# Hybrid encoder layer on one core: the triangular solve, the recurrence and the gates each run one attention later, and the weighted sums one tile later

## The chip, the cores and the metric

The kernel runs on one core of one Trainium2 chip. The metric is the device time of one execution in microseconds (us), lower is better; the time of a kernel is the median of its runs. TensorE (PE) multiplies, VectorE (DVE) and ScalarE (ACT) do the elementwise work, GpSimd (POOL) does a little and issues DMAs, SyncE (SP) issues the other DMAs and the transposes that go through DMA.

## The reference

One layer of a hybrid streaming encoder over T = 1088 tokens (1024 prompt tokens and 64 sample tokens), D = 1024. Four branches read one projection `u @ w_in`: fox (attention with a forgetting bias), diff (difference of two softmaxes), sb (stick-breaking attention: a reversed cumulative sum over the keys) and gdn (gated DeltaNet: a unit-triangular solve in each 64-token chunk, then a recurrence over the chunks). Their outputs are gated and merged, and an output projection and a feed-forward network follow.

```
x = x + W_out( sum_b sigmoid(gate_b(u)) * P_b(branch_b(u)) ),  u = rms_norm(x)
x = x + swiglu(rms_norm(x));  y = rms_norm(x)
# gdn: sol = triangular_solve(m + I, rhs) of every chunk; then, chunk after chunk,
v_new = u_i - kc_i @ S
o     = (q_i * exp(g_i)) @ S + a_i @ v_new
S     = S * exp(g_last) + (k_i * exp(g_last - g_i))^T @ v_new
```

The outputs are y, the new keys and values of the three attentions, and the new state of gdn, for both token groups.

## The kernel before

Every large product is made of f16 pairs (a high and a low part), so it costs three matmuls. The tokens are cut into 9 tiles of at most 128 rows; an attention goes over 2 pairs of heads and, in each, over the tiles in the order `QORD` (7, 6, 5, 4, 3, 2, 8, 1, 0), the longest rows of keys first. For one tile the sequence is: load the queries (`load_q`, a DMA transpose), score matmuls (`scores`, tile `psc`), softmax or stick-breaking on ACT and DVE, a DMA transpose of the probabilities (`p_tiles`, `pt<-st`, line 447), then the weighted sums (`pv_pair`, tile `pv`, lines 462 to 473; in diff `diff_out`, tile `po`).

Between the scores and the weighted sums of a tile the code calls `fill(us)` (lines 503 to 515). It takes other work from two lists. `dense` holds matmul work that waits for nothing: units of 24 matmuls, either of a projection (tile `pd`, lines 165 to 167, 256 columns each) or of a gate (tile `pgs`, lines 183 to 185, up to 364 columns each, copied out by ACT as `ths` and written to memory). There are 96 gate units, in 16 generators' worth of weights. `side` holds a chain of small steps: `gdn_solve` (lines 861 to 890, 30 steps of forward substitution on DVE, tiles `X` and `tmpx`) or `gdn_seq` (lines 896 to 1040, the recurrence over 17 chunks: for each tile a preparation, `py` to `kc`, and for each chunk `vn`, `vh`, `pds`, `S`, `Sh`, `Sl`, `pks`, then `pog` and `osg`, which goes to memory as `od_gdn`).

The stages before: sb attention, with the rest of the fox projection and the diff projection as fill and the solve as side chain; fox attention, with gates as fill and the recurrence as side chain; diff attention, with the rest of the gates as fill. The merges follow: for each branch its outputs (`oT`), its weights (`wbh`, `wbl`) and 24 products (`ptb`) that are multiplied by the tanh of the gates (`thg`) and added up. Their pool `brp` is opened before diff attention. Then come the output projection and the feed-forward network, which the change does not touch.

The order in which an engine gets its instructions is not that of the code: a scheduler simulates a timeline and places them. A statement inside `tc.issue_after(x)` is placed no earlier than x.

## Time and profile before

| | us |
|---|---|
| median of 3 runs | 1852.74 (1850.4 to 1865.82) |
| the profiled execution | 1846.53 |
| its span | 1844.7 |
| PE busy | 1731.3 (94%) |
| DVE busy | 1253.2 (68%) |
| ACT busy | 864.1 (47%) |
| first score of sb / fox / diff | 301.4 / 489.5 / 640.4 |
| last gate matmul, last merge matmul | 957.7, 1064.7 |

The profiled execution lies 1.8 us beside its span and 6.2 us under the median. The last two lines are points in the timeline of the trace, counted from the start of the span. A busy TensorE is not one at its peak: matmuls are pipelined, and the records overlap, so the granted clock and the time from start to start have to be read beside the busy time.

### The profile page before, as it was taken

The page shows a single profiled execution, that of the slowest core. Times are in us where ns is not written, and L with a number is a line of the kernel's source. Part 1 is how long each engine was busy: PE and PEld are TensorE (multiplying, and loading weights), DVE is VectorE, ACT ScalarE, POOL GpSimd, SP SyncE. Part 2 cuts the span into 40 slices and gives each one's busy share as a digit, 9 for nine tenths or more (in the row PEclk, how much of TensorE's full clock was granted, in tenths as well). Part 3 has the DMA queues.
Part 4 walks back from the last instruction along what each step waited for, and adds up shares of the span by engine and source line. Part 5 has one row for each costly group of instructions (what it writes and reads, how often), then busy time and mean ns, then how long its engine had stood idle before and what let it go on. Part 6 is the DMA issues. An engine that isn't in the chain of part 4 may idle for free.

```text
span 1844.7 us, 36720 instructions
## 1 busy us (share of the span) xinstructions
PE 1731.3 (94%) x14364; PEld 1226.5 (66%) x14364; DVE 1253.2 (68%) x2589; ACT 864.1 (47%) x1819; POOL 302.9 (16%) x445
## 2 busy tenths in 40 slices
PE   7999887798898899999998899999999999999997
PEld 5678775675565566666565588777758668577573
DVE  7558874899766576877757886757546456465455
ACT  6335555888755554655646533423314224132132
POOL 2113221001222222232334620000000000000002
PEclk9999998899999999999999999999999999999999
DMA  6267689989899975664949746412212112112113
GB/s 227 50 107 200 209 245 167 217 185 208 181 193 214 191 154 143 147 163 102 251 133 285 209 132 108 101 52 58 70 35 78 37 48 81 35 35 69 35 47 103
DMA packets 412157, 244.60 MB, mean 133 GB/s; under 512 B 266146, under 2 KB 389502, under 8 KB 411916
## 3 DMA queue, kind: packets, MB, share of 16 engines
q1 hardware_dynamic: 398944, 205.67, 47.1%
q0 software_dynamic: 13040, 36.60, 7.4%
q8 instruction: 112, 1.84, 0.4%
q14 instruction: 61, 0.50, 0.1%
HBM read 123.39 MB, written 60.81 MB: 100 GB/s over the span
## 4 chain that ended last, share of the span: by engine, by line
PE 66%; DMA 13%; DVE 11%; issue 5%; ACT 3%; POOL 1%; SPq 1%; DVEq 0%; POOLq 0%; ACTq 0%
PE po L1432 12%; PE pgs L185 5%; PE pgs L183 5%; PE pgs L184 5%; DMA pt<-st 4%; PE pb L1316 3%; PE pb L1315 3%; PE pb L1317 3%; PE pc L1316 2%; PE pc L1317 2%; PE pa L1317 2%; PE pc L1315 2%; PE pa L1316 2%; PE pa L1315 2%; PE psc L456 2%
## 5 line engine op out<-in xcount | busy, mean ns | idle before, releaser
L183 PE MATMUL pgs<-u,wh 128*128 128x364 f16 (+1 forms) x768 | 245.3, 319 | 2.7 <-ACT ths L61 2.7
L185 PE MATMUL pgs<-u,wl 128*128 128x364 f16 (+1 forms) x768 | 245.5, 320 | 0.0
L184 PE MATMUL pgs<-u,wh 128*128 128x364 f16 (+1 forms) x768 | 245.4, 320 | 0.0
L1432 PE MATMUL po<-wh,hT 128*128 128x512 f16 (+1 forms) x792 | 238.1, 380 | 0.6 <-DVE x2a L64 0.6
L1432 PEld LDWEIGHTS <-hT 128*128 128x128 f16 (+1 forms) x1188 | 109.2, 99 | 120.0 <-issue 7.6
L64 DVE SCALAR_TENSOR_TENSOR x2a<-po,x2a 128x512 f32<-128x512 f32 x108 | 74.5, 690 | 140.2 <-PE po L1432 140.0
L61 ACT ACTIVATE wh<-w32f 128x1024 f16<-128x1024 f32 (+1 forms) x90 | 80.3, 926 | 160.6 <-PE po L1432 111.7
L1315 PE MATMUL pb<-X,wh 128*128 128x288 f16 (+1 forms) x528 | 147.1, 279 | 2.5 <-DMA X<-nsh 2.2
L64 DVE SCALAR_TENSOR_TENSOR wl<-w32f,wh 128x1024 f16<-128x1024 f32 (+1 forms) x90 | 94.7, 1066 | 79.8 <-ACT wh L61 79.7
L1316 PE MATMUL pb<-X,wh 128*128 128x288 f16 (+1 forms) x528 | 147.2, 279 | 0.3 <-DMA X<-nsl 0.3
L1317 PE MATMUL pb<-X,wl 128*128 128x256 f16 (+1 forms) x528 | 146.3, 279 | 0.0
L1432 PE MATMUL po<-wl,hT 128*128 128x512 f16 (+1 forms) x396 | 142.0, 379 | 0.0
L1315 PEld LDWEIGHTS <-wh 128*128 128x128 f16 x1232 | 120.5, 98 | 31.0 <-issue 2.3
L1316 PEld LDWEIGHTS <-wh 128*128 128x128 f16 x1232 | 120.5, 98 | 30.0 <-issue 2.4
L1317 PEld LDWEIGHTS <-wl 128*128 128x128 f16 x1232 | 120.5, 98 | 27.2 <-issue 0.9
L165 PE MATMUL pd<-wh,u 128*128 128x256 f16 (+1 forms) x448 | 125.6, 280 | 4.0 <-DVE qs L64 2.6
L167 PE MATMUL pd<-wh,u 128*128 128x256 f16 (+1 forms) x448 | 125.0, 279 | 0.0
L166 PE MATMUL pd<-wl,u 128*128 128x256 f16 (+1 forms) x448 | 125.0, 279 | 0.0
L184 PEld LDWEIGHTS <-wh 128*128 128x128 f16 x912 | 89.8, 98 | 51.9 <-issue 4.1
L185 PEld LDWEIGHTS <-wl 128*128 128x128 f16 x912 | 89.6, 98 | 51.0 <-issue 2.6
L183 PEld LDWEIGHTS <-wh 128*128 128x128 f16 x912 | 89.7, 98 | 50.4 <-issue 1.5
L71 POOL TENSOR_SCALAR fss<-fss 128x1 f32<-128x1 f32 (+1 forms) x9 | 2.0, 219 | 660.3 <-ACT fsq L1461 660.3
(393 smaller groups left out, 4642.7 us busy)
## 6 DMA issues: line engine op xcount, KB each, us to landing
w<-in_w_in_dram SPq DMA_DIRECT2D x56, 512.0 KB, 4.8
w32f<-in_w_ffn_gate_dram SPq DMA_DIRECT2D x20, 512.0 KB, 5.0
w32f<-in_w_ffn_up_dram SPq DMA_DIRECT2D x20, 512.0 KB, 4.0
w32f<-in_w_ffn_down_dram SPq DMA_DIRECT2D x20, 512.0 KB, 4.0
xt<-in_x_prompt_dram SPq DMA_DIRECT2D x8, 512.0 KB, 6.8
wb<-in_w_branch_dram SPq DMA_DIRECT2D x8, 512.0 KB, 4.8
w<-in_w_out_dram SPq DMA_DIRECT2D x8, 512.0 KB, 5.8
x2a<-in_x_prompt_dram SPq DMA_DIRECT2D x8, 512.0 KB, 6.7
```

Of the source, the lines that this page charges most:

```text
L61: return act.activation(out, in_, AF.Copy, scale=scale)
L64: return vec.scalar_tensor_tensor(out=out, in0=in0, scalar=s, in1=in1, op0=op0, op1=op1)
L165: pe.matmul(ps[:n, :N], lhsT=a, rhs=wh[:, k, :N], start=(k == 0), stop=False)
L166: pe.matmul(ps[:n, :N], lhsT=a, rhs=wl[:, k, :N], start=False, stop=False)
L167: pe.matmul(ps[:n, :N], lhsT=b, rhs=wh[:, k, :N], start=False, stop=(k == K - 1))
L183: pe.matmul(ps[:, :n], lhsT=a, rhs=xh[:, k, off:off + n], start=(k == 0), stop=False)
L184: pe.matmul(ps[:, :n], lhsT=a, rhs=xl[:, k, off:off + n], start=False, stop=False)
L185: mm = pe.matmul(ps[:, :n], lhsT=b, rhs=xh[:, k, off:off + n], start=False, stop=(k == K - 1))
L1315: pe.matmul(ps[:, :n], lhsT=wh[:, k], rhs=xh_, start=(start and k == 0), stop=False, skip_group_check=not start)
L1316: pe.matmul(ps[:, :n], lhsT=wh[:, k], rhs=xl_, start=False, stop=False, skip_group_check=not start)
L1317: mm = pe.matmul(ps[:, :n], lhsT=wl[:, k], rhs=xh_, start=False, stop=(k == 3), skip_group_check=not start)
L1432: pe.matmul(ps[h * n:h * n + n], lhsT=hts[k + h][:, a, tk:tk + n], rhs=w[:, k + h], start=(k == 0 and a == 0 and w is wh), stop=(k + nh >= ...
```

## The change

Three things change.

- The weighted sums of a tile are held back (`behind_scores`) and issued behind the last score matmul of the next tile; there are 6 buffers for transposed probabilities instead of 4, and `tiles_of` requests the queries of the next tile, and the keys and values of the next pair, one tile ahead.
- The side work moves one attention on. Sb attention is filled with the rest of the fox projection and gates and has no side chain; fox attention is filled with the diff projection and gates and has the solve; diff attention has the rest of the gates and the recurrence. The merges' pool is opened only when the recurrence's pool has been closed.
- The matrix that the solve reads, `nd`, is stored in three 32 by 32 blocks: 51 smaller writes instead of 17, and one contiguous load instead of two strided ones.

```diff
-FILL_SB, FILL_FOX, FILL_DIFF, FILL_GDN = 0.0143, 0.006, 0.0155, 8
+FILL_SB, FILL_FOX, FILL_DIFF, FILL_GDN = 0.0143, 0.0085, 0.0155, 8
...
-        pt = at.tile([P, 16, P], F16, tag="pt", name="pt", bufs=4)
+        pt = at.tile([P, 16, P], F16, tag="pt", name="pt", bufs=6)
...
+    def tiles_of(b):
+
+        units = [(pair, t) for pair in range(2) for t in QORD]
+        kv, q = {}, {}
+        for k in range(len(units)):
+            for m in range(k, min(k + 2, len(units))):
+                pair, t = units[m]
+                if pair not in kv:
+                    kv[pair] = load_kv(b, pair)
+                if m not in q:
+                    q[m] = load_q(b, pair, t, rows(t))
+            pair, t = units[k]
+            yield pair, t, q.pop(k), kv[pair]
+
+    held = []
+
+    def behind_scores(mm, run):
+
+        if held:
+            with tc.issue_after(mm.ins) if mm is not None else ExitStack():
+                held.pop()()
+        if run is not None:
+            held.append(run)
...
-        for pair in range(2):
-            kT, vt = load_kv("sb", pair)
-            for t in QORD:
+        for pair, t, qt, (kT, vt) in tiles_of("sb"):
                 n, kc, W, vl = qgeom(t)
-                qt = load_q("sb", pair, t, n)
                 pts = []
...
-                    sb_mark[0] = stt(sv[:n, 1, :W], z[:n, :W], PS, sv[:n, 0, :W], ALU.mult, ALU.subtract)
+                    stt(sv[:n, 1, :W], z[:n, :W], PS, sv[:n, 0, :W], ALU.mult, ALU.subtract)
                     pts.append(tr())
+                behind_scores(mm, lambda a=(pair, t, n, vt, vl, pts): pv_pair("sb", *a))
                 fill(FILL_SB * W)
-                pv_pair("sb", pair, t, n, vt, vl, pts)
+        behind_scores(None, None)
 
...
+                    at_mark[0] = stt(sv[:n, 1, :W], s[:n, :W], mn[:n, 3:4], sv[:n, 0, :W], ALU.mult, ALU.subtract)
                     pts.append(tr())
+                behind_scores(mm, lambda a=(pair, t, n, vt, vl, pts): pv_pair("fox", *a))
                 fill(FILL_FOX * W)
-                pv_pair("fox", pair, t, n, vt, vl, pts)
+        behind_scores(None, None)
 
...
+                    behind_scores(mm, lambda a=(pair, t, n, nb, vl, vt, hp, pt, o32): diff_out(*a))
                     fill(FILL_DIFF * W / 2)
-                    diff_out(pair, t, n, nb, vl, vt, hp, pt, o32)
+        behind_scores(None, None)
...
-    nd = tc.dram_tile([18, NH, 64, 64], F32, name="nd")
+    nd = tc.dram_tile([18, NH, 3, 32, 32], F32, name="nd")
...
-                gps.dma_start(nd[2 * t + c].rearrange("h j i -> j h i"), n32[64 * c:64 * c + 64])
+                for b, (j0, i0) in enumerate(((0, 0), (32, 32), (0, 32))):
+                    gps.dma_start(nd[2 * t + c, :, b].rearrange("h j i -> j h i"),
+                                  n32[64 * c + j0:64 * c + j0 + 32, :, i0:i0 + 32])
...
-            for q in range(2):
-                sl = slice(32 * q, 32 * q + 32)
-                gps.dma_start(X[:, q], nd[0:17, :, sl, sl].rearrange("n h j i -> (n h) j i"))
+            gps.dma_start(X.rearrange("p b j i -> p b (j i)"), nd[0:17, :, 0:2].rearrange("n h b j i -> (n h) b (j i)"))
...
-                behind = tc.issue_after(sb_mark[0].ins) if j == 1 else ExitStack()
+                behind = tc.issue_after(at_mark[0].ins) if j == 1 else ExitStack()
...
-    def spill_gates(b, sp):
+    def spill_gates(b, sp, d2):
...
-        dense += proj
+        dense += proj[0:2]
...
-        side.append(gdn_solve())
+        dense += [spill_gates(b, sp, d2) for b in gtd for d2 in range(4)]
         attend_sb()
-    drain(dense)
-    drain(side)
-    pj_.close()
+    drain(dense, proj[1])
+    drain(dense, dense[0])
     cb_ = ExitStack()
     cb = cb_.enter_context(tc.tile_pool(name="cb", bufs=1, side="right", reuse_waits="tile"))
+    dense.insert(0, proj[2])
+    side.append(gdn_solve())
+    attend_fox()
+    drain(dense, proj[2])
+    drain(side)
+    cb_.close()
+    pj_.close()
     gd_ = ExitStack()
     g3 = gd_.enter_context(tc.tile_pool(name="gp3", bufs=1, side="right", reuse_waits="tile"))
-    dense += [spill_gates(b, sp) for b in gtd]
     side.append(gdn_seq(g3))
-    attend_fox()
+    attend_diff()
     drain(side)
     gd_.close()
-    cb_.close()
+    drain(dense)
+    ap_.close()
     br_ = ExitStack()
     brp = br_.enter_context(tc.tile_pool(name="br", bufs=1, side="right", reuse_waits="tile"))
-    attend_diff()
-    drain(dense)
-    ap_.close()
```

Counted in the order of the changed kernel, 5 gate units stand before sb's first score, 31 between sb's first and last score, 5 in fox attention and the other 55 behind diff's first score. Three places show the move.

VectorE, in the middle of sb attention of the kernel before (`cu`, `z` and `st` are a head's stick-breaking, `X` and `tmpx` the solve, `ks` the projection of diff's keys):

```order
L541 SCALAR_TENSOR_TENSOR cu_4536<-cu_4536,e_4535 128x512
L64 SCALAR_TENSOR_TENSOR st_4310<-z_4291,st_4310 128x640
L67 TENSOR_TENSOR tmpx_3733<-X_3732 68x60
L67 TENSOR_TENSOR z_4534<-z_4534,cu_4536 128x512
L71 TENSOR_SCALAR cu_4556<-z_4554 128x512
L64 SCALAR_TENSOR_TENSOR os_4261<-pv_4224,os_4261 128x128
L67 TENSOR_TENSOR X_3732<-X_3732,tmpx_3733 68x2x30
L67 TENSOR_TENSOR tmpx_3733<-X_3732 68x116
L64 SCALAR_TENSOR_TENSOR ks_4778<-e32_4775,ks_4778 128x8x32 x2
L67 TENSOR_TENSOR X_3732<-X_3732,tmpx_3733 68x2x2x29
```

and VectorE of the changed kernel, where the solve begins, in fox attention (`ISA` is fox's row maximum, `s` and `st` its softmax):

```order
L64 SCALAR_TENSOR_TENSOR st_6906<-s_6892,mn_6893,st_6906 128x640
L67 TENSOR_TENSOR tmpx_6483<-X_6482 68x60
L64 SCALAR_TENSOR_TENSOR st_7036<-s_7026,mn_7027,st_7036 128x512
L67 TENSOR_TENSOR X_6482<-X_6482,tmpx_6483 68x2x30
L64 SCALAR_TENSOR_TENSOR ks_7013<-e32_7010,ks_7013 128x8x32 x2
L67 TENSOR_TENSOR tmpx_6483<-X_6482 68x116
L591 ISA s_7165,mn_7166<-psc_7167,ckb_6308 128x384
L591 ISA mn_7166 128x1
L591 ISA s_7180,mn_7181<-psc_7182,ckb_6308 128x384
L591 ISA mn_7181 128x1
```

The solve's steps and the copies of diff's projection stand between the softmax steps of fox and no longer between those of sb.

TensorE at the end of the recurrence, before (`pog` is its last output, `psc` scores of diff, `pgs` a gate):

```order
L1017 LDWEIGHTS rec2b_9342
L1017 MATMUL pog_9380<-vh1_6340,rec2b_9342 64x64
L1018 LDWEIGHTS rec2b_9342
L1018 MATMUL pog_9380<-vh1_6340,rec2b_9342 64x64
L456 LDWEIGHTS qt_11871
L456 MATMUL psc_11878<-kT_11160,qt_11871 128x128
L458 LDWEIGHTS identb_75
L458 MATMUL psc_11878<-mk_diff_83,identb_75 128x128
L456 LDWEIGHTS qt_11871
L456 MATMUL psc_11888<-kT_11160,qt_11871 128x512
L184 LDWEIGHTS wh_13076
L184 MATMUL pgs_13226<-u1_103,wh_13076 128x360
```

and TensorE of the changed kernel at its last gate matmuls (`pu` belongs to the recurrence's tile 5; tiles 6 and 7 are still to come):

```order
L183 MATMUL pgs_13790<-u1_103,wh_13640 128x360
L184 LDWEIGHTS wh_13640
L184 MATMUL pgs_13790<-u1_103,wh_13640 128x360
L185 LDWEIGHTS wl_13641
L185 MATMUL pgs_13790<-u1_103,wl_13641 128x360
L456 LDWEIGHTS qt_13060
L456 MATMUL psc_13204<-kT_11714,qt_13060 128x256
L458 LDWEIGHTS identb_75
L458 MATMUL psc_13204<-mk_diff_83,identb_75 128x128
L997 LDWEIGHTS ttbd1_8773
L997 MATMUL pu_11007<-rec1b_11001,ttbd1_8773 128x64
```

No gate is left behind this point: before, gates stood on both sides of the recurrence's end, and now the rest of tile 5 and the whole of tiles 6 and 7 stand behind the last gate, and the first merge product (`ptb`) behind them.

ScalarE at the end of the recurrence, before (`osg` is the recurrence's last output, `wbh` the first merge weights, `p` a softmax of diff):

```order
L61 ACTIVATE ths_13289<-pgs_13264 128x364
L61 ACTIVATE osg_9626<-ztg_9378 128x256
L61 ACTIVATE t32_11855<-po_11842 128x64
L614 ACTIVATE sq_11858<-o32_11655 128x128
L655 ACTIVATE p_11887,sm16_11873<-psc_11888,sm16_11873 128x512
L655 ACTIVATE p_11887,sm16_11873<-psc_11891,sm16_11873 128x128
L61 ACTIVATE ths_13317<-pgs_13292 128x364
L61 ACTIVATE wbh_13807<-wb32_13809 128x1024
L1145 ACT_TABLE_LOAD
L1145 ACTIVATE thg_13817<-thg_13817 128x364
```

and of the changed kernel:

```order
L61 ACTIVATE u0_11653<-pu_11627 128x256
L61 ACTIVATE kc_11655<-pk_11628 128x512
L61 ACTIVATE vh0_8781<-vn_11672 64x256
L61 ACTIVATE Sh_11710<-S32p_8785 128x256
L61 ACTIVATE vh1_8783<-vn_11780 64x256
L1050 ACTIVATE sqo_11852<-pog_11660 128x256
L61 ACTIVATE osg_11860<-ztg_11658 128x256
L61 ACTIVATE wbh_13840<-wb32_13842 128x1024
L61 ACTIVATE wbh_13840<-wb32_13846 128x1024
L61 ACTIVATE wbh_14117<-wb32_14119 128x1024
```

The first merge weights stand behind `osg` of tile 7 in both; now nothing of diff and no gate stands beside them. GpSimd in the changed kernel:

```order
L1060 DMA od_gdn_349<-osg_11581 128x512
L1047 DMA out_p_gdn_state_dram<-S32p_8785 64x4x64
L72 TENSOR_SCALAR sso_11854<-sso_11854 128x4
L67 TENSOR_TENSOR sso_11854<-sso_11854,mhb_79 128x4
L1060 DMA od_gdn_349<-osg_11860 128x512
L1148 DMA oT_13837<-od_sb_342 128x2x1088 x2
L1148 DMA oT_14114<-od_fox_343 128x2x1088 x2
```

The loads of the branch outputs (`oT`) stand behind the write of the last `osg`.

## Rows read from the trace of the kernel before

**Rows 1.** The page: span, part 1 (busy time, share of the span and instructions of each engine) and the engines' shares of the chain that ended last.

```profile
span 1844.7 us, 36720 instructions
...
PE 1731.3 (94%) x14364; PEld 1226.5 (66%) x14364; DVE 1253.2 (68%) x2589; ACT 864.1 (47%) x1819; POOL 302.9 (16%) x445
...
PE 66%; DMA 13%; DVE 11%; issue 5%; ACT 3%; POOL 1%; SPq 1%; DVEq 0%; POOLq 0%; ACTq 0%
...
```

**Rows 2.** Windows by stage, core 0: the stretch, its length, busy us of each engine (instructions), mean granted TensorE clock, DMA share, GB/s. The stretches are: before the first score of sb; sb attention; between; fox attention; between; diff attention to the last gate matmul; the merges.

```profile
...
core 0: us, PE busy (x) PEld busy (x) DVE busy (x) ACT busy (x) POOL busy (x), PEclk, DMA share, GB/s
229.00:301.40 72.40, 57.20 (x524) 49.79 (x522) 41.35 (x78) 35.70 (x76) 18.75 (x25) 0.90 0.95 212
301.40:483.20 181.80, 158.24 (x1466) 113.04 (x1467) 159.48 (x278) 151.29 (x292) 22.87 (x34) 0.94 0.95 197
483.20:489.50 6.30, 6.30 (x61) 3.97 (x60) 5.51 (x13) 5.00 (x17) 1.58 (x3) 1.00 0.84 236
489.50:626.40 136.90, 122.34 (x1365) 78.58 (x1363) 92.04 (x296) 78.87 (x181) 29.48 (x48) 0.95 0.98 194
626.40:640.40 14.00, 12.13 (x125) 8.04 (x124) 5.79 (x16) 5.73 (x18) 3.01 (x5) 1.00 1.03 238
640.40:957.70 317.30, 311.61 (x2780) 203.47 (x2781) 229.49 (x708) 175.79 (x463) 89.19 (x143) 1.00 0.64 154
957.70:1064.70 107.00, 89.76 (x554) 54.24 (x552) 85.51 (x141) 60.75 (x121) 56.91 (x53) 0.98 0.80 234
...
```

**Rows 3.** What TensorE waited for from 229 to 640 us: us in total, times, longest us.

```profile
...
PE pv L468 <- DMA pt<-st: 24.4, 11, 6.7
PE psc L456 <- DMA qt<-qd_sb: 9.9, 1, 9.9
PE psc L456 <- DMA qt<-qd_fox: 5.8, 2, 3.5
...
```

**Rows 4.** ScalarE's groups of instructions in sb attention (301.4 to 483.2 us): busy us, mean ns | idle before.

```profile
...
L61 ACT ACTIVATE e<-pd 128x256 f32<-128x256 f32 (+1 forms) x18 | 6.9, 383 | 0.1
L61 ACT ACTIVATE ks<-e 128x512 f16<-128x512 f32 (+1 forms) x9 | 5.7, 629 | 0.0
L61 ACT ACTIVATE ths<-pgs 128x364 f32<-128x364 f32 (+1 forms) x12 | 5.6, 470 | 2.0 <-PE pgs L185 2.0
L61 ACT ACTIVATE qs<-pd 128x512 f16<-128x512 f32 (+1 forms) x7 | 4.1, 587 | 7.2 <-PE pd L167 7.2
...
```

**Rows 5.** VectorE's groups in the same stretch.

```profile
...
L67 DVE TENSOR_TENSOR X<-X,tmpx 68x60 f32<-68x60 f32 (+14 forms) x30 | 14.6, 488 | 0.1
L67 DVE TENSOR_TENSOR tmpx<-X 68x60 f32<-68x60 f32 (+14 forms) x30 | 14.5, 482 | 0.1
...
L64 DVE SCALAR_TENSOR_TENSOR ks<-e,ks 128x256 f16<-128x256 f32 (+1 forms) x18 | 6.8, 415 | 0.0
L64 DVE SCALAR_TENSOR_TENSOR qs<-pd,qs 128x256 f16<-128x256 f32 (+1 forms) x14 | 5.3, 417 | 5.1 <-ACT qs L61 5.1
...
```

**Rows 6.** TensorE's groups in the same stretch.

```profile
...
L165 PE MATMUL pd<-wh,u 128*128 128x256 f16 (+1 forms) x184 | 52.2, 284 | 2.6 <-DVE qs L64 2.6
...
L183 PE MATMUL pgs<-u,wh 128*128 128x364 f16 (+1 forms) x102 | 32.9, 322 | 2.7 <-ACT ths L61 2.7
...
```

**Rows 7.** TensorE's group of line 183 in diff attention (640.4 to 957.7 us).

```profile
...
L183 PE MATMUL pgs<-u,wh 128*128 128x364 f16 (+1 forms) x506 | 160.5, 317 | 0.0
...
```

**Rows 8.** Timeline of TensorE in the recurrence's last chunk: start us, duration us.

```profile
...
870.44 0.32 PE L183 MATMUL pgs<-u,wh 128*128 128x360 f16 x1
870.59 0.32 PE L184 MATMUL pgs<-u,wh 128*128 128x360 f16 x1
...
873.62 0.48 PE L1011 MATMUL pds<-vh,rec2b 128*128 128x64 f16 x11
...
```

**Rows 9.** Timeline of VectorE about the recurrence's last two chunks: start us, duration us.

```profile
...
863.27 0.41 DVE L64 SCALAR_TENSOR_TENSOR S32p<-pds,S 128x256 f32<-128x256 f32 x1
...
863.80 0.42 DVE L67 TENSOR_TENSOR S<-S32p,eg 128x256 f32<-128x256 f32 x1
...
864.97 0.43 DVE L64 SCALAR_TENSOR_TENSOR Sl<-S32p,Sh 128x256 f16<-128x256 f32 x1
...
869.23 0.43 DVE L64 SCALAR_TENSOR_TENSOR vn<-pks,u 64x256 f32<-64x256 f32 x1 [0.33 <-PE pks L999]
...
870.13 0.42 DVE L67 TENSOR_TENSOR vh<-vn,vh 64x256 f16<-64x256 f32 x1 [0.29 <-ACT vh L61]
...
876.20 0.41 DVE L1032 TENSOR_REDUCE sso<-sqo 128x4 f32<-128x256 f32 x1
...
```

**Rows 10.** VectorE's groups in diff attention that prepare a tile of the recurrence.

```profile
...
L67 DVE TENSOR_TENSOR kc<-pk,kc 64x512 f16<-64x512 f32 x5 | 3.5, 694 | 1.9 <-ACT kc L61 1.8
...
L955 DVE COPY tt<-px 32x128 f32<-32x128 f32 x10 | 2.8, 283 | 5.0 <-PE px L954 4.7
...
```

**Rows 11.** Timeline of GpSimd (POOL) behind the recurrence's last matmul: start us, duration us.

```profile
...
876.71 1.16 POOL L72 TENSOR_SCALAR sso<-sso 128x4 f32<-128x4 f32 x1 [1.19 <-DVE sm L67]
877.95 1.96 POOL L67 TENSOR_TENSOR sso<-sso,mhb 128x4 f32<-128x4 f32 x1
...
```

**Rows 12.** DMA issues: queue, operation, count, KB each, median us from issue to landing.

```profile
...
oT<-od_sb POOLq DMA_DIRECT2D x2, 544.0 KB, 5.8
...
```

**Rows 13.** Windows of 50 us: the one in which sb attention begins (columns as in rows 2).

```profile
...
300.00:350.00 50.00, 37.26 (x350) 27.68 (x351) 35.81 (x43) 38.95 (x58) 3.80 (x2) 0.84 1.13 199
...
```

More of the change, by code (lines that the diff above doesn't have):

```diff
@@ L356, in put_v @@
         r = slice(r0, r0 + n)
-        vs = pj.tile([P, NH, 2, 64], F16, tag="vs", name="vs", bufs=4)
+        vs = pj.tile([P, NH, 2, 64], F16, tag="vs", name="vs", bufs=3)
         s4 = src.rearrange("p (h e) -> p h e", h=NH)
@@ L365, in put_q @@
         if b == "diff":
-            qs = pj.tile([P, 8, 2, 2, 32], F16, tag="qs", name="qs", bufs=5)
+            qs = pj.tile([P, 8, 2, 2, 32], F16, tag="qs", name="qs", bufs=4)
             pv = src.rearrange("p (a e) -> p a e", e=32)
@@ L371, in put_q @@
         else:
-            qs = pj.tile([P, NH, 2, 2, 64], F16, tag="qs", name="qs", bufs=5)
+            qs = pj.tile([P, NH, 2, 2, 64], F16, tag="qs", name="qs", bufs=4)
             pv = src.rearrange("p (a e) -> p a e", e=64)
@@ L455, in scores @@
         last = mask is None and not two
-        pe.matmul(ps[:n, :w], lhsT=q0, rhs=kk[:, col:col + w], start=True, stop=last)
+        mm = pe.matmul(ps[:n, :w], lhsT=q0, rhs=kk[:, col:col + w], start=True, stop=last)
         if mask is not None:
@@ L532, in attend_sb @@
                         diag = W - n - c0 if c0 + w == W else None
-                        scores(ps, n, w, qt[:, 2 * hp, :n], qt[:, 2 * hp + 1, :n], kT[hp], kc + c0,
+                        mm = scores(ps, n, w, qt[:, 2 * hp, :n], qt[:, 2 * hp + 1, :n], kT[hp], kc + c0,
                                mk_sb if diag is not None else None, diag)
@@ L567, in attend_fox @@
                         diag = W - n - c0 if c0 + w == W else None
-                        scores(ps, n, w, qt[:, 2 * hp, :n], qt[:, 2 * hp + 1, :n], kT[hp], kc + c0,
+                        mm = scores(ps, n, w, qt[:, 2 * hp, :n], qt[:, 2 * hp + 1, :n], kT[hp], kc + c0,
                                mk_fox if diag is not None else None, diag)
@@ L627, in attend_diff @@
     def attend_diff():
-        for pair in range(2):
-            kT, vt = load_kv("diff", pair)
-            for t in QORD:
+        for pair, t, qt, (kT, vt) in tiles_of("diff"):
                 n, kc, W, vl = qgeom(t)
@@ L633, in attend_diff @@
                 o32 = at.tile([P, 2, 64], F32, tag="o32", name="o32", bufs=3)
-                qt = load_q("diff", pair, t, n)
                 for hp in range(2):
@@ L1042, in tile_hybrid_encoder @@
     bidx = {"fox": 0, "diff": 1, "sb": 2, "gdn": 3}
-    def spill_gates(b, sp):
+    def spill_gates(b, sp, d2):
         j = bidx[b]
-        for d2 in range(4):
-            wu = load_unit([(w_in, 0, OFF_GATE + j * D + d2 * BW, BW)], BW)
-            for m in range(2):
-                d = 2 * d2 + m
-                for off, n in PIECES:
-                    pg = pd("pgs")
-                    gemm_a(pg, wu, m * P, uh, ul, off, n, KD)
-                    th = sp.tile([P, 364], F32, tag="ths", name="ths", bufs=2)
-                    with tc.high_priority():
-                        acopy(th[:, :n], pg[:, :n], 0.5 * IWS)
-                    gps.dma_start(gtd[b][d * P:(d + 1) * P, off:off + n], th[:, :n])
-                    yield 3.7
+        wu = load_unit([(w_in, 0, OFF_GATE + j * D + d2 * BW, BW)], BW)
+        for m in range(2):
+            d = 2 * d2 + m
+            for off, n in PIECES:
+                pg = pd("pgs")
+                gemm_a(pg, wu, m * P, uh, ul, off, n, KD)
+                th = sp.tile([P, 364], F32, tag="ths", name="ths", bufs=2)
+                with tc.high_priority():
+                    acopy(th[:, :n], pg[:, :n], 0.5 * IWS)
+                gps.dma_start(gtd[b][d * P:(d + 1) * P, off:off + n], th[:, :n])
+                yield 3.7
     with tc.tile_pool(name="gp1", bufs=1, side="right", reuse_waits="tile") as g1p:
```

20 lines of the change are left out of this document (9 added, 11 removed).

## The prediction

> **What bounds the kernel now.** The page first: TensorE is busy for 1731.3 of 1844.7 us, and two thirds of the chain that ended last lie on it [rows 1]. So the question is where TensorE loses time around the change, and the view that tells is the windows by stage [rows 2]; the waits, the groups and the timeline then give the prices.
>
> The price of matmul work: in a gate unit one matmul of 360 columns starts 0.15 us after the other [rows 8], so 0.42 ns a column at full clock, and a gate unit of 24 matmuls costs 3.65 us, a projection unit of 24 at 256 columns 2.6 us. By this price I counted the columns of all matmuls of a stretch, as an estimate, before in the trace and for the change in its order. Of sb attention's 181.8 us [rows 2], 150 are such work: 32 are lost. Fox attention has 111 of 136.9 us: 26 lost. Diff attention has 287 of 317.3: 30 lost, over a long stretch. The losses have three forms. TensorE idles 23.6 us in sb attention and 14.6 in fox (length less busy time, [rows 2]); the weighted sums' wait for transposed probabilities is 24.4 us in 11 waits, and the queries' first landings cost 9.9 and 5.8 [rows 3]; and behind idle time the granted clock is lower, 0.90 to 0.95 over these stretches, against 1.00 in diff attention [rows 2]. In sb attention VectorE is busy 159.5 of 181.8 us (88%) and ScalarE 151.3, and in fox they are at 92.0 and 78.9 of 136.9 [rows 2]: in sb they are close to setting the pace, in fox not.
>
> **The change part by part.** I follow the profiled execution, 1846.5 us, which lies 6.2 under the median of the runs.
>
> 1. *Up to sb's first score* (301.4). Five gate units come in ahead of it and some projection work moves with them, 13 us of columns more. They stand where TensorE waits 9.9 us for the queries [rows 3]. 301.4 + 13 - 9.9 is 304.5; I take **305**. Ends: 302 (the lower clock vanishes too) and 314 (the wait stays).
>
> 2. *Sb attention.* The solve leaves: X and tmpx are 29.1 us of VectorE [rows 5]. So do diff's projections: ks and qs 12.1 on VectorE [rows 5] and with vs about 17.8; on ScalarE e, ks, qs 16.7 [rows 4] and with vs about 21. On TensorE 184 of each of three matmuls [rows 6], 23 units, leave, and gate units rise from 102 / 8 = 12.7 [rows 6] to 31, which costs ScalarE 18.3 ths at 0.47 [rows 4], 8.6. The groups of an engine overlap a little (ScalarE's sum to 175, it is busy 151.3), so I count nine tenths: VectorE falls to some 115 us, ScalarE to some 140, TensorE has 140 of columns. Before, the busiest engine had 88% of the stretch; 140 / 0.88 is **158**. The ends are 145 (either engine nearly unbroken) and 175 (today's 32 lost stay). Gain 24, of which 10 is work gone elsewhere. What covers the weighted sums is now the next tile's scores; if ScalarE is late these scores are late, and the wait for pt<-st becomes a wait for a bank of scores. That is why I don't let all the loss vanish.
>
> 3. *Between sb and fox*: 6.3 us [rows 2] become 14.3 of columns (the rest of a fill is drained there): **+8**.
>
> 4. *Fox attention.* The recurrence leaves VectorE (about 20 us of small steps), the solve's 29.1 and the projections' 17.8 arrive, with some weight splits: 92 to about 120. Gates fall, 24 projection units arrive: 128 us of columns. VectorE at 120 doesn't lead, so TensorE does, with a little over half of the 26 us loss, as the queries' 5.8 us and part of the pt waits go: **142**, +5. Ends 131 and 154.
>
> 5. *Between fox and diff*: 14.0 us [rows 2] become nothing: **-14**. So diff's first score comes at 305 + 158 + 14.3 + 142 = 619, 21 earlier than 640.4.
>
> 6. *Diff attention to the last gate*: 506 / 8 = 63.3 gate units [rows 7] become 55: -30.5. Four merge products, 3.5 us, that before stood among the gates are gone. The recurrence is about as long there as before. 317.3 - 34 is **283**: the last gate ends at 902, 56 earlier than 957.7.
>
> 7. *The recurrence's end without cover.* By the order of the change nothing but the recurrence is left for TensorE behind the last gate, apart from the last small diff tiles: the rest of tile 5 and tiles 6 and 7. Before, gates stood on both sides, and the merges followed them without a gap. The chain of a chunk from the rows: vn 0.43, vh 0.42 twice (a high part on ScalarE, a low part on VectorE), pds 0.48, S32p 0.41, S 0.42, the two parts of S 0.43 twice, eight pks about 0.4 [rows 8, 9]: 3.8, with handovers 4.4 us. A tile's preparation: four copies at 0.28 and kc at 0.69 [rows 10], the high parts of the same on ScalarE, two block copies at 0.42, and eight short TensorE steps at about 0.2: 5.7 us. Tiles 6 and 7 are 4 x 4.4 + 2 x 5.7 = 29. The rest of tile 5, two chunks and half a preparation, with diff's last softmaxes beside it: 14. The finish: sso 0.41 [rows 9], 1.16 and 1.96 on GpSimd [rows 11], five more steps at about 0.42, the issues, then the landing of the branch outputs, 5.8 [rows 12]: 14. Together **57**: the first merge product comes at 959, where before the merges proper began at 957.7. Ends: 45 (tile 5 nearly done, loads early) and 71 (5.5 us a chunk, diff's last tiles on VectorE in the way).
>
> 8. *Merges.* 107.0 [rows 2] and the 3.5 us of products done early before, less some 3 for twelve tanh of fox that are now ready: 108. The window in which sb attention begins, behind idle TensorE, has a granted clock of 0.84, 8 us of 50 lost [rows 13]; the merges begin behind 57 us of thin work, so I add 4, between 0 and 8: **112**. The last merge product ends at 1071 instead of 1064.7.
>
> A rule of the Trainium skill speaks to this. Its page "TensorE: Matmul & The Clock Gate", section "HAM oscillation — how this bites in real kernels", says that a TensorE that idles between groups of matmuls falls back to half rate and has to win full rate again. By it all of the merges' beginning would run at the lower of the two levels until the clock rises; the trace agrees that it does behind sb's first wait, and no row shows a stretch as thin as this one.
>
> 9. *nd in blocks, more issues and buffers*: 34 issues more on GpSimd stand ahead of sb attention, where it is busy 18.8 of 72 us [rows 2], and the solve that reads nd starts 170 us later. Nothing, unless a solve step is late; from below nothing too.
>
> The sum: -56 at the last gate, +57 for the uncovered end, +5 in the merges: **+6 us**, 1853 in the profiled sense, and 1859 against the median. The work that is hidden better early is paid back in the recurrence's end, which lost its cover. I say **1859 us: no change** by the measure of 1% (18.5 us).
>
> **The rivals.** *A, faster: the early gains are whole and the end is short.* Sb attention at 145, fox at 131 and the uncovered end at 45, with merges at 108: 13 + 11 + 12 + 4 = 40 less, 1819. For it: 24.4 us of pt waits sit exactly where the change works [rows 3], and the freed VectorE. Against: every one of four terms must go well, and ScalarE is as loaded as TensorE.
>
> *B, slower: the uncovered end is long.* One mechanism: in-order TensorE holds a tile of the recurrence and diff's last weighted sums in one line, so that each waits for the other's VectorE steps. Prepared tiles take turns over two banks, so nothing of tile 7 starts before tile 6's outputs are copied. At 71 us and with 8 for the clock: +18, 1877. It decides from about 70 us between the last gate and the first merge product; a chunk among gates now takes far longer than the 4.4 us I use, which was never seen bare.
>
> *C, slower: the held weighted sums don't do what they are meant for.* Sb and fox keep their losses of 32 and 26 us: 172 and 154, +26 together, 1885. For it: before, the scheduler already put scores of the next head ahead of many weighted sums. Against: VectorE, the busiest engine in sb, loses 45 us of work.
>
> **How the numbers follow.** Chances: my forecast 0.47, A 0.20, B 0.20, C 0.13. The forecast alone reaches from 1840 to 1875. The range has to leave out no more than 2 in 10: it goes from 1824 (half of A) to 1888 (all of B, two thirds of C). Faster by over 1%, below 1834: most of A and a little of the forecast, 0.19. Slower by over 1%, above 1871: B and C mostly, and a little of the forecast, 0.31. Within 1%: 0.50.
>
> **What would show each step.** In the profile after: sb attention about 158 us with VectorE near 115 and ScalarE near 140; no wait of over 5 us for qt<-qd_sb or qt<-qd_fox; pt<-st waits under 10 us in all; diff's first score near 619 and the last gate near 902; then TensorE mostly idle for some 57 us, waiting for vn, vh, S and at last for wbh or oT. If the last gate ends near 902 and the merges begin before 950, step 7 is wrong and the kernel is faster; if diff's first score is still near 640, steps 2 to 5 are wrong and it is slower.

## The result and the profile after

The changed kernel takes 1866.2 us (median of 20 runs) against 1852.7 for the kernel before: a ratio of 1.0075, with a 95% interval of 1.0056 to 1.0094. That is slower, by less than the 1% that was called no change. The profiled execution has a span of 1864.8 us, 20 more than before.

The page of the changed kernel, with the span, the busy time and the engines' shares of the chain, as in [rows 1]:

```profile
span 1864.8 us, 36814 instructions
...
PE 1743.7 (94%) x14364; PEld 1236.5 (66%) x14364; DVE 1252.0 (67%) x2589; ACT 867.2 (47%) x1819; POOL 302.5 (16%) x478
...
PE 54%; DVE 7%; DMA 7%; issue 2%; ACT 2%; POOL 1%; SPq 0%; DVEq 0%; POOLq 0%; ACTq 0%
...
```

The windows by stage of the changed kernel, which answer to [rows 2]: before sb's first score, sb attention, between, fox attention, diff attention to the last gate, from there to the first merge product, the merges:

```profile
...
229.00:310.00 81.00, 69.65 (x579) 54.19 (x577) 41.62 (x78) 35.03 (x78) 30.70 (x48) 0.96 0.93 234
310.00:461.80 151.80, 142.11 (x1217) 89.31 (x1218) 114.00 (x149) 136.97 (x258) 24.47 (x41) 0.98 0.83 174
461.80:476.50 14.70, 14.63 (x133) 9.14 (x131) 8.65 (x26) 8.93 (x32) 3.68 (x6) 1.00 0.55 124
476.50:618.50 142.00, 127.78 (x1348) 97.39 (x1346) 110.44 (x338) 83.82 (x178) 14.85 (x24) 0.98 0.96 212
618.60:907.10 288.50, 280.70 (x2577) 183.15 (x2576) 213.62 (x661) 157.23 (x416) 72.91 (x128) 0.99 0.66 153
907.10:972.00 64.90, 34.44 (x431) 27.51 (x429) 40.64 (x136) 31.62 (x86) 18.64 (x31) 0.54 0.35 101
972.00:1086.90 114.90, 96.97 (x576) 57.85 (x575) 89.67 (x142) 60.39 (x114) 51.01 (x49) 0.95 0.80 244
...
```

Sb attention is 30 us shorter than before, with VectorE at 114 and ScalarE at 137. The row from 907.1 to 972 has no counterpart before: 65 us with a granted clock of 0.54. What TensorE waited for between 229 and 640 us, as in [rows 3]:

```profile
...
PE pv L469 <- DMA pt<-st: 12.9, 10, 2.7
PE pgs L183 <- ACT ths L61: 7.2, 3, 6.3
...
PE psc L456 <- DMA qt<-qd_sb: 1.2, 1, 1.2
...
```

and in those 65 us:

```profile
...
PE ptb L183 <- DMA oT<-od_sb: 11.6, 1, 11.6
PE pds L1031 <- ACT vh L61: 5.7, 6, 1.2
...
PE pks L1018 <- DVE kc L67: 2.8, 2, 1.4
...
```

| | before | predicted | after |
|---|---|---|---|
| first score of sb | 301.4 | 305 | 310.0 |
| sb attention | 181.8 | 158 | 151.8 |
| fox attention | 136.9 | 142 | 142.0 |
| first score of diff | 640.4 | 619 | 618.6 |
| last gate | 957.7 | 902 | 907.1 |
| last gate to first merge product | none | 57 | 64.9 |
| merges | 107.0 | 112 | 114.9 |
| last merge product | 1064.7 | 1071 | 1086.9 |
| from there to the end | 780.0 | | 777.9 |

### The profile page after: what moved, and what is told of

It reads as the page before. It is cut to its first block, busy times and chain, and to the rows that moved or that the text cites. A ratio compares the mean times of both kernels' runs of the same rounds, so it can differ in the third digit from the quotient of the medians.

```text
span 1864.8 us, 36814 instructions
## 1 busy us (share of the span) xinstructions
PE 1743.7 (94%) x14364; PEld 1236.5 (66%) x14364; DVE 1252.0 (67%) x2589; ACT 867.2 (47%) x1819; POOL 302.5 (16%) x478
## 4 chain that ended last, share of the span: by engine, by line
PE 54%; DVE 7%; DMA 7%; issue 2%; ACT 2%; POOL 1%; SPq 0%; DVEq 0%; POOLq 0%; ACTq 0%
PE po L1454 12%; PE pgs L183 3%; PE pgs L185 3%; PE pgs L184 3%; PE pb L1338 3%; PE pb L1337 3%; PE pb L1339 3%; DMA pt<-st 3%; PE pc L1338 2%; PE pc L1339 2%; PE pa L1339 2%; PE pc L1337 2%; PE pa L1338 2%; PE pa L1337 2%; DMA w<-in_w_out_dram 1%
## 5 line engine op out<-in xcount | busy, mean ns | idle before, releaser
L1454 PE MATMUL po<-wl,hT 128*128 128x512 f16 (+1 forms) x396 | 142.0, 379 | 0.0
L165 PE MATMUL pd<-wh,u 128*128 128x256 f16 (+1 forms) x448 | 123.3, 275 | 7.7 <-ACT e L61 7.1
L167 PE MATMUL pd<-wh,u 128*128 128x256 f16 (+1 forms) x448 | 123.2, 275 | 0.0
```

Source lines behind the costliest of these rows:

```text
L165: pe.matmul(ps[:n, :N], lhsT=a, rhs=wh[:, k, :N], start=(k == 0), stop=False)
L167: pe.matmul(ps[:n, :N], lhsT=b, rhs=wh[:, k, :N], start=False, stop=(k == K - 1))
L1454: pe.matmul(ps[h * n:h * n + n], lhsT=hts[k + h][:, a, tk:tk + n], rhs=w[:, k + h], start=(k == 0 and a == 0 and w is wh), stop=(k + nh >= ...
```

## The experiments

Times are medians; the kernel before ran beside each at 1852.5 to 1856.9.

**Is the end slow because cover is missing there?** e1 holds back 12 gate units for the end.

```diff
-                    pe.matmul(py[up_, 32 * h:32 * h + 32], lhsT=t32[lo_, h, 32:64], rhs=t11[lo_, h], start=True, stop=True)
+                    seq_mark[t] = pe.matmul(py[up_, 32 * h:32 * h + 32], lhsT=t32[lo_, h, 32:64], rhs=t11[lo_, h], start=True, stop=True)
...
+    late = dense[-2:]
+    del dense[-2:]
     attend_diff()
     drain(side)
+    drain(dense)
+    with tc.issue_after(seq_mark[6].ins):
+        drain(late)
     gd_.close()
-    drain(dense)
...
```

> The changed kernel, but the last 12 of the 96 gate units are held back on TensorE until the first product (py) of the recurrence's tile 6. Theory 'end without cover': the 65 us between the last gate and the first merge product are lost because no work is left beside the recurrence; 12 units x 3.65 us = 44 us of gates move into it and leave diff attention, so the first merge product comes near 930 instead of 972, the granted clock there is near 1.00, and the time is 1814 to 1834 us. Rival 'the chain sets the pace': from diff's first score to its end the recurrence needs its time wherever the gates stand; with fewer gates ahead TensorE idles ahead of tile 6 instead, the first merge product stays within 10 us of 972, and the time is 1855 to 1875 us.

Measured: 1879.2 us, ratio 1.0136 (1.0112 to 1.0160), 13 more than the changed kernel. The first merge product comes at 985, 366 us behind diff's first score. The windows of e1 before the held gates (two of 40 us) and with them:

```profile
...
840.00:880.00 40.00, 26.69 (x282) 18.40 (x279) 32.47 (x104) 21.26 (x59) 6.95 (x13) 0.62 0.53 125
880.00:920.00 40.00, 30.23 (x267) 20.41 (x267) 35.78 (x150) 24.13 (x77) 12.82 (x21) 0.57 0.57 105
920.00:966.00 46.00, 46.00 (x423) 30.44 (x422) 12.69 (x35) 17.74 (x43) 10.71 (x19) 1.00 0.31 104
...
```

The held gates run at full clock, but in the 80 us ahead of them TensorE now idles for 23, at a granted clock of about 0.6. My theory of the missing cover falls. The rival named the right thing but not its size: the first merge product is 13 us behind 972, and the time 4 us above its range. The pace of the recurrence tells why. Starts of `vn` in the changed kernel (VectorE, first chunk of tiles 3, 4, 6 and 7, and the second chunk of tile 6 in the fourth row; start us, duration us):

```profile
829.62 0.41 DVE L64 SCALAR_TENSOR_TENSOR vn<-pks,u 64x256 f32<-64x256 f32 x1
...
872.09 0.42 DVE L64 SCALAR_TENSOR_TENSOR vn<-pks,u 64x256 f32<-64x256 f32 x1
...
935.42 0.42 DVE L64 SCALAR_TENSOR_TENSOR vn<-pks,u 64x256 f32<-64x256 f32 x1 [0.73 <-PE pks L1019]
...
939.75 0.43 DVE L64 SCALAR_TENSOR_TENSOR vn<-pks,u 64x256 f32<-64x256 f32 x1 [0.63 <-PE pks L1019]
...
952.92 0.42 DVE L64 SCALAR_TENSOR_TENSOR vn<-pks,u 64x256 f32<-64x256 f32 x1 [0.73 <-PE pks L1019]
```

Among gates and diff's scores and softmax a tile takes 42.5 us (829.62 to 872.09), bare 17.5 (935.42 to 952.92); there the second chunk starts 4.33 behind the first. The windows of these two tiles:

```profile
...
829.60:872.10 42.50, 42.50 (x412) 28.29 (x410) 31.39 (x93) 22.20 (x61) 9.85 (x17) 1.00 0.59 140
935.40:952.90 17.50, 10.85 (x136) 8.77 (x137) 8.51 (x21) 10.51 (x23) 1.86 (x3) 0.50 0.44 159
```

e1 holds the two cases between them. From `vn` of tile 4 (862.24) to that of tile 5 (893.70) diff runs and no gate does; from tile 6 (930.31) to tile 7 (966.94) the held gates run, and diff's last weighted sum has started just before (930.27):

```profile
...
862.20:893.70 31.50, 20.91 (x197) 13.88 (x196) 27.93 (x98) 17.92 (x52) 4.97 (x9) 0.50 0.46 94
930.30:966.90 36.60, 36.60 (x333) 23.92 (x333) 9.68 (x26) 14.84 (x35) 7.94 (x14) 1.00 0.28 98
...
```

With diff alone a tile takes 31.5 us, at a granted clock of 0.50; with gates alone 36.6, at full clock and with VectorE busy for 9.7 us only. Either alone gives most of the slow pace. Gates that are moved to the end fill TensorE there, but they also slow the recurrence that they were to cover.

**The same from the other side: less fill in sb, more in diff.** e11:

```diff
-FILL_SB, FILL_FOX, FILL_DIFF, FILL_GDN = 0.0143, 0.0085, 0.0155, 8
+FILL_SB, FILL_FOX, FILL_DIFF, FILL_GDN = 0.0085, 0.0085, 0.0155, 8
```

> The changed kernel with a smaller fill in sb attention (0.0085 for 0.0143): by its order 13 gate units instead of 28 stand among sb's scores, 16 instead of 5 in fox attention and 62 instead of 55 behind diff's first score. Theory 'the chain sets the pace': what counts is when diff attention starts; sb attention falls to ScalarE's 140 to 148 us, fox rises by 11 units to 170 to 180, diff's first score comes near 634 instead of 619 and the first merge product about 350 us behind it, 975 to 990, so the time is 1868 to 1884 us. Rival 'end without cover': 7 units more, 26 us, stand where cover is missing, and the time falls to 1850 to 1860 us.

Measured: 1866.0 us, ratio 1.0075 (1.0048 to 1.0101), the same as the changed kernel, between the two ranges. The edit moved more than gates: 23 of the 27 units of diff's projection came into sb attention, which takes 161.6 us instead of 140 to 148, and fox shrinks to 126, so that diff's first score comes already at 603.4. Windows of e11 from there to the last gate, and on to the first merge product:

```profile
...
603.40:934.00 330.60, 322.19 (x3007) 210.57 (x3006) 242.28 (x757) 178.42 (x478) 88.83 (x151) 0.98 0.63 152
934.00:969.90 35.90, 15.27 (x212) 12.55 (x211) 17.17 (x40) 16.01 (x35) 9.51 (x15) 0.56 0.25 84
...
```

The bare end shrinks from 65 to 36 us, and the stretch from diff's first score to the last gate grows from 288.5 to 330.6. The first merge product stands 366 us behind diff's first score; in the changed kernel it is 353.

**Only the recurrence's start moved.** e9 is the kernel before with:

```diff
-    side.append(gdn_seq(g3))
-    attend_fox()
+    attend_fox()
+    side.append(gdn_seq(g3))
+    attend_diff()
     drain(side)
     gd_.close()
     cb_.close()
+    drain(dense)
     br_ = ExitStack()
     brp = br_.enter_context(tc.tile_pool(name="br", bufs=1, side="right", reuse_waits="tile"))
-    attend_diff()
-    drain(dense)
     ap_.close()
```

> The kernel before with one thing changed: the recurrence starts in diff attention instead of fox attention, and the merges' pool opens behind it. By its order gates stand on TensorE up to the end of the recurrence (4 units behind it), so there is no end without cover. Theory 'the chain sets the pace' (the recurrence needs some 350 us from diff's first score, wherever gates stand): first merge product near 640 + 353 = 993, TensorE idles inside diff attention, the time is 1880 to 1900 us. Rival 'end without cover' (only the missing gates at the end cost time): TensorE's work before the merges is the same as in the kernel before, the first merge product comes near 970 (12 us for the branch outputs' load), the time is 1860 to 1872 us.

Measured: 1857.0 us, ratio 1.0014 (0.9984 to 1.0045): no difference, and both ranges missed. Windows of e9, diff attention to the last gate and the merges:

```profile
...
616.00:958.80 342.80, 338.70 (x3177) 221.46 (x3175) 248.67 (x767) 188.83 (x499) 94.96 (x161) 1.00 0.62 150
959.00:1078.50 119.50, 97.97 (x576) 58.41 (x575) 90.51 (x141) 63.62 (x123) 52.77 (x50) 0.93 0.78 242
...
```

TensorE is busy 338.7 of 342.8 us behind diff's first score, and the recurrence ends at 944, 328 us behind it, inside that work. The 353 I expected was too long: its first chunk ran at 549, in fox. So here a late start cost nothing, with 338.7 busy us of TensorE's work behind it; in the changed kernel there are 280.7 to the last gate.

**What sets the pace?** e13 cuts the gates drawn from diff on to an eighth (`gemm_a(..., light[0])` with 1 for 8 blocks of depth).

> The changed kernel with the gate units that are drawn from diff attention on cut to 3 of their 24 matmuls (an eighth of the product's depth, so these gates and y are wrong). In the changed kernel a tile of the recurrence takes 44 us among gates and 17.5 us bare. Theory 'handovers queue behind gates': each time the recurrence hands something to TensorE, its matmuls stand 2.5 to 3 us behind gate matmuls in the in-order queue; with an eighth of them the pace falls to 18 to 28 us a tile, and the first merge product comes 180 to 260 us behind diff's first score instead of 353. Rival 'VectorE and ScalarE, which diff's softmax keeps busy, set the pace': it stays at 35 us a tile or more, the first merge product 300 us or more behind diff's first score.

Measured in a single run: 1836.0 us; the first merge product at 942, 321 us behind diff's first score. A tile takes 39 to 40 us up to the last of the thin gates, at 789, and 30 to 36 behind it, until diff's scores end. Its window in diff, and TensorE's waits from 640 to 900:

```profile
...
640.00:942.00 302.00, 186.88 (x1794) 125.00 (x1794) 232.20 (x758) 175.60 (x482) 85.25 (x146) 0.64 0.65 153
...
```

```profile
...
PE po L626 <- DMA pt<-st: 34.0, 18, 5.2
PE psc L456 <- ACT p L674: 16.1, 23, 3.4
...
```

The theory's 18 to 28 us a tile are missed, and the first merge product comes where the rival put it. 48 units' worth of matmuls are gone, 176 us at 3.65, and the kernel is only 30 us faster than the changed one. TensorE waits for diff's transposed probabilities and softmax, and VectorE is busy 232 of 302 us. But the granted clock is 0.64 here, where the changed kernel has 0.99: the run takes the full clock away together with the gates, and how much of the 30 to 36 us is diff's softmax and how much the slower TensorE it doesn't show. Nor does it say that gates cost the recurrence little: by the tile of e1 that has gates alone (36.6 us against 17.5 bare) they cost it 19 us where nothing else runs.

**Which part gives the early gain?** e4 is the changed kernel without held sums:

```diff
-                behind_scores(mm, lambda a=(pair, t, n, vt, vl, pts): pv_pair("sb", *a))
                 fill(FILL_SB * W)
+                pv_pair("sb", pair, t, n, vt, vl, pts)
...
```

> The changed kernel with the weighted sums issued behind their own tile's fill, as before the change; the new schedule, 6 buffers and the requests ahead stay. Theory 'the early gain is mostly the schedule's': with VectorE freed, sb attention stays at 152 to 162 us and fox at 142 to 150, the time is 1866 to 1878 us. Rival 'the early gain is the held sums'': the pt waits come back to 20 us or more, sb attention takes 168 us or more, and the time is 1882 us or more.

Measured: 1872.6 us, ratio 1.0110 (1.0062 to 1.0159). Sb attention is 151.2 us and fox 146.2, the waits for transposed probabilities 16.5 (the profile is that of its slowest run, 1887.4 us): the gain in sb does not come from holding. Whether holding helps here is not settled, as the intervals overlap.

e3 puts the other parts into the schedule of before (the statements at the bottom of the file and `FILL_FOX` as before, `pt` bufs=4). What stays with them, here and in e12, is that the change also has one buffer less for projected queries (4) and values (3):

> The schedule of the kernel before (solve in sb, recurrence and gates from fox on, merges' pool open before diff) with the other part of the change: weighted sums held behind the next tile's scores, queries and keys requested a tile ahead, nd in blocks; 4 buffers of transposed probabilities, since 6 don't fit beside the recurrence's pool and fox's. Theory 'end without cover': the early gain comes partly from this part (24.4 us of pt waits, 15.7 us of waits for queries), and the end keeps its gates: sb attention 165 to 175 us, fox 125 to 132, diff's first score 618 to 630, no gap between gates and merges, time 1828 to 1843 us. Rival 'the early gain is VectorE's': what made sb shorter is the solve's 29 us and the projections' 18 that left VectorE; then sb attention stays at 177 or more, and the time is 1843 us or more.

Measured: 1842.1 us, ratio 0.9934 (0.9909 to 0.9959). Sb attention 173.0, but fox 147.5 and diff's first score at 636: the early gain is small. The time is inside the theory's range, fox and diff's first score are not.

e12 is e3 with the edit of e4:

> As e3 (the schedule of before, queries and keys requested a tile ahead, nd in blocks), but with the weighted sums issued behind their own tile's fill as before the change. Theory 'holding the weighted sums is what e3 gains from': pt waits stay near 24 us and the time is 1847 to 1855 us, 5 to 13 above e3's 1842. Rival 'the requests ahead are': sb's first score stays near 300, and the time is 1838 to 1845 us.

Measured: 1825.6 us, ratio 0.9855 (0.9835 to 0.9875), the fastest of all, and outside both ranges. Holding costs 16 us in this schedule. Part of it is one wait of e3 in diff attention, of 10.6 us, for a held sum's probabilities, which e12 doesn't have:

```profile
...
PE po L626 <- DMA pt<-st: 10.6, 1, 10.6
...
```

Windows of e12: sb, fox, diff to the last gate, merges:

```profile
...
308.10:480.90 172.80, 153.74 (x1438) 109.06 (x1437) 156.16 (x268) 150.21 (x293) 22.78 (x36) 0.97 0.89 200
485.60:628.70 143.10, 131.39 (x1410) 84.04 (x1410) 93.63 (x290) 80.18 (x181) 30.48 (x50) 0.94 0.95 197
640.30:938.50 298.20, 296.02 (x2689) 194.48 (x2690) 227.02 (x701) 173.09 (x457) 80.61 (x138) 1.00 0.64 161
938.50:1048.50 110.00, 93.67 (x571) 56.39 (x569) 86.67 (x147) 62.14 (x125) 58.73 (x56) 0.97 0.77 230
...
```

No bare end, and TensorE idles 2 us of 298 in diff.

e14 and e15 put one part each into the kernel before: the held sums (`behind_scores` as in the diff above), and the requests ahead (`tiles_of`).

> The kernel before, with the weighted sums held behind the next tile's scores and nothing else changed. After e3 (1842) and e12 (1826), which differ in this alone: theory 'holding brings nothing to the old schedule', time 1850 to 1866 us. Rival 'holding helps where queries come late': the pt waits fall below 15 us and the time is 1838 to 1846 us.

Measured: 1861.4 us, ratio 1.0047 (1.0018 to 1.0076). The waits for transposed probabilities are 24.7 us: holding takes none away, as the theory had it.

> The kernel before, with queries and the next pair's keys and values requested a tile ahead and nothing else changed (nd as before). Theory 'the requests ahead are e12's whole gain': time 1824 to 1834 us. Rival 'nd in blocks is part of it' (17 issues of 64 KB in 256-byte pieces and two strided loads come back): 1836 to 1848 us.

Measured: 1859.4 us, ratio 1.0033 (1.0014 to 1.0051). Both ranges missed. So the third part, nd in blocks, by itself (e16, the hunks of `nd` and X's load from the diff above):

> The kernel before, with nd in three blocks (51 smaller writes, one contiguous load) and nothing else changed. e15 had the requests ahead without it (1859), e12 has both and smaller buffers for projected queries and values (1826). Theory 'nd in blocks is e12's gain': by its order some 36 gate units stand ahead of diff's first score, as in e12, instead of 33; the time is 1826 to 1840 us. Rival 'the two only help together': 1846 to 1858 us. What the prediction said of it was nothing from either side.

Measured: 1837.4 us, ratio 0.9903 (0.9871 to 0.9934). The part that I had priced at nothing gains 1%. The load of X, before and in e16 (DMA issues: count, KB each, median us to landing):

```profile
...
X<-nd POOLq DMA_DIRECT2D x2, 272.0 KB, 18.3
...
```

```profile
...
X<-nd POOLq DMA_DIRECT2D x1, 544.0 KB, 8.4
...
```

The windows of 10 us from 285 to 305 of the kernel before:

```profile
...
285.00:295.00 10.00, 6.55 (x60) 5.63 (x58) 4.13 (x8) 3.77 (x6) 2.98 (x1) 0.95 1.23 164
295.00:305.00 10.00, 3.57 (x15) 1.79 (x16) 0.69 (x1) 2.05 (x3) 0.00 (x0) 0.54 1.20 65
...
```

and of e16:

```profile
...
285.00:295.00 10.00, 9.75 (x90) 8.51 (x89) 6.41 (x14) 5.71 (x10) 2.19 (x4) 1.00 0.81 232
295.00:305.00 10.00, 9.06 (x83) 7.87 (x81) 2.49 (x7) 1.79 (x3) 0.00 (x0) 1.00 1.10 241
...
```

Before, from 295 to 305 us the DMA engines have a share of 1.20 and move 65 GB/s, with the first strided load under way (issued at 284.85; the second follows at 306.14), and TensorE is busy 3.6 of 10 us at a granted clock of 0.54; this is where it waits 9.9 us for sb's first queries [rows 3]. In e16 a share of 1.10 moves 241 GB/s there. The packet records of the traces agree: in these 10 us a packet of 256 bytes on the hardware queues takes 103 ns on average before and 29 in e16, and before it took 18 from 285 to 290, ahead of the load's first packet. e15 (first row) keeps the old layout in another order and has the hole in the same place; e12 (second row) has the blocks and hasn't:

```profile
...
295.00:305.00 10.00, 1.40 (x5) 0.43 (x4) 0.76 (x2) 0.70 (x2) 0.00 (x0) 0.63 1.28 67
...
```

```profile
...
295.00:305.00 10.00, 8.95 (x68) 7.42 (x69) 3.84 (x11) 2.22 (x5) 0.00 (x0) 0.83 1.09 284
...
```

So the hole comes with the strided load. How much of the 18 us it makes, no run shows, as the layout changes the order too: in e16 65 projection units instead of 60 stand ahead of sb's first score, which comes at 308.4 instead of 301.4, 36 gate units instead of 33 ahead of diff's first score, and the waits for transposed probabilities are 16.9 us instead of 24.4. A kernel with the load alone elsewhere was not run on the old layout.

**The 5 us ahead of sb.** In the changed kernel a gate write takes 13 us to land, and ScalarE and TensorE wait. GpSimd's timeline and ScalarE's wait:

```profile
...
285.49 1.12 POOL L580 DMA_DIRECT2D ckb<-ckd  x2 [3.52 <-DVE wl L64]
286.60 0.56 POOL L891 DMA_DIRECT2D X<-nd  x1
288.60 1.11 POOL L1075 DMA_DIRECT2D gtd_sb<-ths  x2 [1.44 <-ACT ths L61]
302.42 1.10 POOL L1075 DMA_DIRECT2D gtd_sb<-ths  x2 [12.71 <-ACT ths L61]
```

```profile
...
ACT ths L61 <- DMA gtd_sb<-ths: 13.0, 1, 13.0
...
```

e6 moves X's load behind sb's first outputs, e7 fox's `ckb` loads too:

```diff
-        gps.dma_start(od[b][pair, :, :, t * P:t * P + n], os_[:, :, :n])
+        od_mark[0] = gps.dma_start(od[b][pair, :, :, t * P:t * P + n], os_[:, :, :n])
...
+            with tc.issue_after(od_mark[0].ins):
                 gps.dma_start(X.rearrange(...
...
+                    with tc.issue_after(od_mark[0].ins):
                         for hp in range(2):
                             gps.dma_start(ckb[:, hp], ckd[2 * pair + hp].partition_broadcast(P))
```

> The changed kernel, but the load of the solve's matrix (X from nd) stands on GpSimd's queue behind sb attention's first output writes and no longer ahead of the first gate writes. Theory: the 13.0 us that ScalarE waits for the gate write to land ahead of sb, and TensorE's 6.3 us behind it, are this load's (14.5 us to landing, issued 2 us ahead of the write): the wait goes, sb's first score comes near 304 instead of 310, and the time is 4 to 8 us shorter, 1858 to 1862 us. Rival 'the DMA engines are full there whatever stands ahead' (DMA share 0.93): the write still takes 10 us or more, the first score stays within 2 us of 310, and the time within 3 us of 1866.

Measured: 1868.3 us, ratio 1.0074 (1.0049 to 1.0100), first score at 311.7, ScalarE still waits 14.6 us: the load of X in its new layout is not the cause.

> The changed kernel with fox's broadcast loads (ckb, 672 KB each, two of them issued 3 us ahead of the first gate writes) and X's load both behind sb attention's first output writes on GpSimd's queue. Theory: the gate write that takes 13 us ahead of sb waits for these loads' data; it lands in under 6 us, ScalarE's 13 us and TensorE's 6.3 us go, sb's first score comes near 304 instead of 310, and the time is 1857 to 1863 us (if fox doesn't wait for ckb). Rival: the write is slow for another reason, ScalarE still waits 10 us or more and the first score stays at 308 or later.

Measured: 1858.4 us, ratio 1.0029 (1.0011 to 1.0048), first score at 303.9, the wait gone. The broadcast loads are enough to cause it: with X's load alone moved the wait stays, with both moved it goes, and the changed kernel is 8 us faster, with intervals that don't meet.

## Why the prediction was right, and where not

The range held the time, and the forecast of no change, a little slower, came true. It did so with a right account of the stages and a partly wrong account of the causes. That 1859 lies so near 1866 is partly luck: sb attention came out 6 us shorter than its price and the other terms 22 us longer together, so that the last merge product comes 16 us late (1086.9 for 1071). And the profiled run of the kernel before happens to lie 6.2 us under its median: by the profiled runs the forecast is 13 us short (1853 for 1866.5), by the medians 7.

- *Step 1* (305): 310.0. I had priced the gates ahead of sb as matmuls alone; their write stood behind the `ckb` loads that the new order pulls ahead (e7).
- *Step 2* (158): 151.8, with the engines as worked out (VectorE 115 and 114, ScalarE 140 and 137). The quotient was off by one (140 / 0.88 is 159). Of my 31 gate units 3 stand behind sb's last score, in step 3.
- *Steps 3 to 5*: 14.7, 142.0 and 618.6, as predicted. The pt waits fell to 12.9 us, not under 10.
- *Step 6* (283): 288.5.
- *Step 7* (57): 64.9. The chunk was right (4.4, measured 4.33), the preparation too short: a tile took 17.5 us where 2 x 4.4 + 5.7 is 14.5, 6 us for two tiles. The rest of tile 5 took some 18 for 14, the finish 12 for 14. But the reason was wrong. "Lost its cover" says that gates at the end would help; e1 shows that they don't, as beside them the recurrence itself goes at 36.6 us a tile instead of 17.5. In the change's schedule, with all gates, the recurrence needs some 350 us from diff's first score to the first merge product wherever the gates stand (348 in e7, 353, 362 in e4, 366 in e1 and e11), and the change leaves TensorE less work than that behind diff's first score.
- *Step 8* (112): 114.9.
- *Step 9* (nothing): wrong. nd in blocks, with the order that comes with it, takes 18 us off the kernel before (12 to 24 by the interval of e16). My bound "from below nothing too" was taken without asking what the strided load does to the queries that land beside it, though [rows 3] shows their 9.9 us and the load is issued at 284.85, 17 us ahead of sb's first score.
- *The attribution of the early gain*: steps 1 and 2 count as the schedule's what nd and the requests ahead give in the old schedule too (sb attention is 173 us in e3 and e12, 9 of the 30 us). The sum came out because the stages were priced by their engines and not by the parts of the change.
- *The rivals*: A fell on all four of its terms. B was near: its place was right, and 65 us is just below the point of 70 from which it decides; its mechanism was not tested. C fell as to the time (sb lost 12 us, not 32), though not in its suspicion of the held sums: no run shows a gain from holding that is clear of its interval, and in the old schedule it costs 16 us.
- *The rule of the clock*: the trace agrees, for a short while. In the bare end the granted clock is 0.54; in the first 15 us of the merges it is 0.84, so that the lower of the two levels (1.2 GHz) reaches some 5 us into them, and their whole stretch has 0.95 against 0.98 [rows 2].

Put together by the runs: 1853 before; 1837 with nd in blocks; 1826 with the requests ahead as well and smaller projection buffers; 1842 with held sums; 1866 with the new schedule and 6 buffers. The steps don't add up in any order (the requests alone cost 6 us), and each gives the scheduler another order. Left open: a schedule that starts the recurrence beside fox and diff's projection at once; it was not tried.

## What to carry to other kernels

A long chain of small steps that runs beside other work has two paces, one among it and one alone; when it is moved, compare its length at the slower pace with the work that is left beside it, and don't expect that work moved to its end is free: it slows the chain there. Split a change into its parts before it is judged: here two parts together gained 1.5%, and the held sums and the schedule that came with them cost 2.2% (1826 to 1866 us). A strided load of small pieces can be paid by a transfer that lands beside it, so look at bytes per second beside the DMA share where a load is late.
